# Copies of a head norm's roots one half tile ahead of their transposes, in a kernel of two transformer blocks

## The chip, the cores and the metric

The kernel runs on one core of a Trainium2 chip. The metric is device time in microseconds (us), the median of some runs. Engines are named as the profile names them: PE is TensorE (matmuls and transposes; PEld are its weight loads, which overlap the matmuls), DVE is VectorE, ACT is ScalarE, POOL is GpSimd, SP is SyncE, which issues most DMAs.

## What is computed

The reference is a first block (a causal convolution branch and an RWKV-7 branch, gated and added) and then a second block of two attention layers, each followed by a feed-forward layer with a short convolution; 16 meta tokens and 512 tokens of width 1024, batch 1, float32. The change touches the attention layers, above all the second (layer B), a differential attention. Its queries and keys are normed head by head:

```python
q1, q2 = jnp.split(h @ w_q, 2, axis=-1)
q1 = rms_norm(q1.reshape(B, Tp, N_HEADS, B_HEAD_DIM), gq)      # 8 heads of 64
q2 = rms_norm(q2.reshape(B, Tp, N_HEADS, B_HEAD_DIM), gq)
k1 = rms_norm(k1.reshape(B, Tp, N_HEADS, B_HEAD_DIM), kn_b)    # k2 the same
def attn_map(qb, kk):
    lg = jnp.einsum('bqhd,bshd->bhqs', qb, kk) * scale + bias
    return jax.nn.softmax(jnp.where(mask, lg, NEG_INF), axis=-1)
a = attn_map(q1b, k1) - lam * attn_map(q2b, k2)
```

The first attention layer (layer A) picks 256 keys for each query by an index score and has heads of 128.

## The kernel before

Activations lie transposed: 128 channels on the partitions, T = 528 tokens along the free axis, in two halves of 264 columns (`HALVES`). A projection (`gemm`, L1089) takes a weight tile of 128 x 1024 floats, which a DMA brings (`wst`), ACT casts to a high part (`wh`), and POOL subtracts to a low part (`wl`). Three products for each of 8 k tiles and each half, 48 matmuls of 264 columns, go to PSUM banks `g` or `pt`; DVE evacuates them.

Only PE's order is written by the program. The class `Weave` keeps a planner's clock: every matmul adds its cost. Before each main product `mm3` calls `tick`, which lets those streams (generators) go on that are due. A stream yields either a delay on that clock (a value of `LAT2`; in layer B `LATB` replaces some, `hd` by 8) or a condition. The other engines' instructions are ordered by a scheduler, by readiness and priority.

A head norm is such a stream (`head_norm`, L1202). It squares two tiles (ACT), sums the squares per head with small matmuls, and takes the reciprocal root (DVE, then a power on POOL), all in a tile `hn` of 88 tokens x 24 values. Then, for each of four half tiles, the roots have to come back along the tokens: with heads of 64, ACT first widens them into `hs` (88 x 384, one buffer), three transposes on PE bring them into a PSUM bank `lg` (two buffers), and DVE multiplies the tile by the gain and the bank. With heads of 128 (layer A) there is no `hs`. The only delay between half tiles is `part` (0.3 or 0.4) between the two tiles.

In layer B four query norms run while the query, key and value projections go on. Then, for each of four pairs of heads `t`, key and value projections are main products, the key norm is a stream of `keys`, and eight attention units (`unit_b`) and one for the meta tokens wait for the marks of q, k and v of that pair. Before the projections of pair `t` from 2 on, `pe.finish(*units[t - 2])` lets PE's plan wait until the units of pair t - 2 are through. In what follows q0 to q3 and k0 to k3 are the four query and key norms.

Of the kernel before, what the change touches and what calls it, by code (L numbers as in the profile page):

```python
# [22 lines left out]
TH = T // 2  # L23
# [624 lines left out]
LAT = dict(lora=4, kk=4, bonus=5, scale=4, am=1.3, inv=34, tf=8.5, merge=2.5, hop=1.5, state=3, gn=14, pivot=40, norm=60)  # L648


LAT2 = dict(acc=3, rstd=2.5, evac=2.5, sq=3, hd=6, part=0.3, soft_a=6, soft_b=4, av=1.6, qn=7, back=5, small=18, dve=1.4, rl=1.8)

LATB = dict(sq=2.5, hd=8, part=0.4, av=1.6, small=12, evac=2)
DEPTH_A, DEPTH_B = 3, 3
# [384 lines left out]
class Block2:  # L1039
# [95 lines left out]
    def rstd(self, acc, r):  # L1135

        K, nc = self.K, self.nc
        n = T // 6
        yield LAT2["acc"]
        p = self.lg()  # L1140
# [4 lines left out]
        K.rsqrt(s, s)  # L1145
        yield LAT2["rstd"]
        for j, sl in enumerate(self.HALVES):
# [23 lines left out]
    def sums(self, st):  # L1171

        K, nc = self.K, self.nc
        yield LAT2["acc"]
        p = self.lg()
# [14 lines left out]
    def start(self, rx, rb):  # L1190
        K, nc = self.K, self.nc
        M0 = N_META
        yield LAT2["rstd"]
        p = self.po()
# [7 lines left out]
    def head_norm(self, xs, width, gcol, key):  # L1202


        K, pe = self.K, self.K.pe
        n = T // 6
        per = P // width
        sel = K.k("ones")[:, 0:1] if per == 1 else K.k("bones")[:, 0:P:width]
        sqs = []
        for x in xs:  # L1210
            sqs.append(K.slot("sq"))
            K.act(sqs[-1], x, AF.Square)
        yield LAT2["sq"]
        w = 6 * per * len(xs)
        p = self.lg()
        for j, sq in enumerate(sqs):
            for b in range(6):
                o = per * (6 * j + b)
                pe.matmul(p[0:n, o:o + per], sq[:, b * n:(b + 1) * n], sel, start=True, stop=True)
        s = self.tl("hn", 2, (n, w))  # L1220
        K.ts(s, p[0:n, :w], 1.0 / width, OP.mult, 1e-6, OP.add)
        K.rsqrt(s, s)
        yield LAT2["hd"]
        for j, x in enumerate(xs):
            for q, sl in enumerate(self.HALVES):
                p = self.lg()[:, :TH]
                o = per * (6 * j + 3 * q)
                if per > 1:
                    r = self.tl("hs", 1, (n, 3, P))
                    K.nc.scalar.copy(r.rearrange("n b (h x) -> n (b h) x", h=per),  # L1230
                                     s[:, o:o + 3 * per, None].to_broadcast([n, 3 * per, width]))
                for b in range(3):
                    pe.transpose(p[:, b * n:(b + 1) * n],
                                 r[:, b] if per > 1 else s[:, o + b:o + b + 1].to_broadcast([n, P]),
                                 K.k("ident")[0:n, 0:n])
                K.stt(x[:, sl], x[:, sl], gcol, p, OP.mult, OP.mult)
            if j + 1 < len(xs):
                yield LAT2["part"]
        pe.mark(key)

    def tl(self, tag, bufs, shape=(P, T), dt=F32):
# [428 lines left out]
    def layer_b(self, hq, acc):  # L1670
# [3 lines left out]
        M0 = N_META  # L1674
        rb = K.slot("rb")
        pq = self.first(self.rstd(acc, rb), (A["w_q_b"][0], hq), (A["w_q_b"][4], hq))
        self.npT = 2
        with self.tc.tile_pool(name="ab", bufs=1, reuse_waits="tile") as self.ap:

            lv = tl("vf", 2)[:, :256]  # L1680
# [27 lines left out]
            for j in range(8):  # L1708
                t, mp = j // 2, j % 2
                p = pq[j] if j < 2 else None  # L1710
                if j == 7:
                    p = self.gemm(A["w_q_b"][t + 4 * mp], hq, both=True, bank=self.pt)
# [42 lines left out]
            acc = K.slot("acc")  # L1755
# [297 lines left out]
```

## Time and profile before

| | |
|---|---|
| median of 3 runs | 2325.27 us (2322.97 to 2329.49) |
| profiled execution | 2321.4 us, span 2319.4 us |
| PE busy | 93% of the span |
| DVE, POOL, ACT busy | 65%, 51%, 38% |
| mean granted PE clock | 0.972 of full speed |
| layer A's key norm | about 983 to 991 us |
| query norms and first key norm of layer B | about 1590 to 1681 us |
| attention units of layer B | about 1690 to 1860 us |

The profile is one execution. Its times are from the span's start. Busy shares are averages over stages with different limits; for a change in one stage the waits of that stage count. A wait in square brackets at a row's end is the idle time of that engine before the row, and what ended it.

### The profile page before, as it was taken

Reading aid. Unit: us, or ns where it says so; the run is one execution under the profiler, and the core shown is the slowest. Engines: PE = TensorE matmul, PEld = TensorE weight load, DVE = VectorE, ACT = ScalarE, POOL = GpSimd, SP = SyncE. Lnnn points to the kernel's source line nnn. Section 1 sums busy time; section 2 is a strip of 40 time slices with the busy share of each in tenths; the row PEclk is TensorE's granted clock in tenths of the full one; section 3 lists DMA queues with packets and bytes.
Section 4 is the critical chain, followed back from the end, with each engine's and each line's share of the span. In section 5 each row is a group of like instructions: output and inputs, shape, how many; then the busy total and the mean of one; then the engine's idle time right before and its main releaser. Section 6 shows DMA issues by size and latency. Waiting matters only on the chain. (4 is left out here: it accounts for less than half of the span.)

```text
span 2319.4 us, 39064 instructions
## 1 busy us (share of the span) xinstructions
PE 2167.0 (93%) x15303; PEld 1897.1 (82%) x15303; DVE 1498.8 (65%) x2693; ACT 889.9 (38%) x1762; POOL 1189.5 (51%) x993
## 2 busy tenths in 40 slices
PE   6999989997999999898999999999888999999999
PEld 4766666665777778897899999999878899988987
DVE  8478986899964377898556616632376766661661
ACT  3423233332243234435433423333375663332331
POOL 5486556475753446435454454465533345454444
PEclk9999999998999999999999999999998999999999
DMA  7422222221244745111022232232111013223223
GB/s 257 162 77 63 64 85 62 66 69 43 84 146 136 243 146 174 61 58 33 29 83 91 72 108 86 84 98 77 56 36 37 19 56 95 82 77 113 88 73 111
DMA packets 110235, 208.85 MB, mean 90 GB/s; under 512 B 45226, under 2 KB 48810, under 8 KB 110051
## 3 DMA queue, kind: packets, MB, share of 16 engines
q1 hardware_dynamic: 107072, 203.26, 28.1%
q10 hardware_dynamic: 2978, 3.10, 0.4%
q8 instruction: 120, 1.97, 0.3%
q14 instruction: 65, 0.52, 0.1%
HBM read 188.43 MB, written 20.57 MB: 90 GB/s over the span
## 5 line engine op out<-in xcount | busy, mean ns | idle before, releaser
L219 POOL TENSOR_TENSOR wl<-wst,wh 128x1024 fp32r<-128x1024 f32 (+4 forms) x315 | 706.9, 2245 | 685.0 <-ACT wh L216 552.6
L75 PE MATMUL g<-hx,wh 128*128 128x264 f32 (+3 forms) x3648 | 877.4, 330 | 0.0
L75 PEld LDWEIGHTS g<-hx,wh 128*128 128x128 f32 x3648 | 616.8, 195 | 53.0 <-issue 8.4
L75 PE MATMUL g<-hx,wl 128*128 128x264 f32 (+3 forms) x1824 | 593.0, 329 | 15.8 <-DVE u L177 7.4
L216 ACT CAST wh<-wst 128x1024 fp32r<-128x1024 f32 (+4 forms) x315 | 304.3, 966 | 375.7 <-PE g L75 207.3
L75 PEld LDWEIGHTS g<-hx,wl 128*128 128x128 f32 x1824 | 351.7, 194 | 42.2 <-DVE u L177 7.9
L177 DVE SCALAR_TENSOR_TENSOR c<-u,vec,c 128x528 f32<-128x528 f32 (+1 forms) x176 | 244.6, 1390 | 83.2 <-ACT c L180 81.6
L75 PE MATMUL pt<-hx,wh 128*128 128x264 f32 (+2 forms) x1504 | 271.9, 283 | 0.0
L177 DVE SCALAR_TENSOR_TENSOR cy<-u,vec,cy 128x512 f32<-128x512 f32 x240 | 234.4, 985 | 3.8
L75 PEld LDWEIGHTS pt<-hx,wh 128*128 128x128 f32 x1504 | 229.6, 188 | 0.0
L75 PE MATMUL pt<-hx,wl 128*128 128x264 f32 (+2 forms) x752 | 207.0, 284 | 9.9 <-DVE u L167 9.8
L75 PEld LDWEIGHTS pt<-hx,wl 128*128 128x128 f32 x752 | 138.9, 188 | 12.2 <-POOL wl L219 8.7
L75 PE MATMUL pt<-f,wh 128*128 128x264 f32 (+1 forms) x528 | 119.5, 320 | 0.0
L75 PE MATMUL g<-f,wh 128*128 128x264 f32 (+1 forms) x528 | 119.5, 320 | 0.0
L1620 ACT CAST f<-t 128x528 fp32r<-128x528 f32 (+1 forms) x44 | 27.6, 627 | 181.1 <-POOL t L167 96.0
L75 PEld LDWEIGHTS g<-f,wh 128*128 128x128 f32 x528 | 87.7, 188 | 7.1
L75 PEld LDWEIGHTS pt<-f,wh 128*128 128x128 f32 x528 | 87.7, 188 | 7.0
L167 POOL TENSOR_TENSOR t<-t,c 128x528 f32<-128x528 f32 (+1 forms) x44 | 57.6, 1310 | 66.9 <-DVE c L177 66.9
L75 PE MATMUL pt<-f,wl 128*128 128x264 f32 (+1 forms) x264 | 84.7, 321 | 2.8 <-POOL wl L219 2.8
L75 PE MATMUL g<-f,wl 128*128 128x264 f32 (+1 forms) x264 | 84.3, 319 | 0.0
L180 ACT ACTIVATE t<-c 128x528 f32<-128x528 f32 (+1 forms) x44 | 28.1, 638 | 139.9 <-DVE c L177 139.9
L167 DVE TENSOR_TENSOR f<-t,f 128x528 fp32r<-128x528 f32 (+1 forms) x44 | 35.4, 805 | 68.8 <-ACT f L1620 68.8
(417 smaller groups left out, 3918.3 us busy)
## 6 DMA issues: line engine op xcount, KB each, us to landing
wst<-in_w_up SPq DMA_DIRECT2D x88, 512.0 KB
wst<-in_w_in SPq DMA_DIRECT2D x66, 512.0 KB
ast<-in_ada_w SPq DMA_DIRECT2D x24, 512.0 KB
wst<-in_w_down SPq DMA_DIRECT2D x32, 384.0 KB
wst<-in_w_down SPq DMA_DIRECT2D x32, 320.0 KB
wst<-in_w_in_a SPq DMA_DIRECT2D x17, 512.0 KB
wst<-in_w_kv_b SPq DMA_DIRECT2D x16, 512.0 KB
wst<-in_w_conv_out SPq DMA_DIRECT2D x8, 512.0 KB
```

The costliest lines, as they stand in the source:

```text
L75: self.nc.tensor.matmul(out, lhsT, rhs, **kw)
L167: (self.nc.vector if eng == "v" else self.nc.gpsimd).tensor_tensor(out, a, b, op)
L177: self.nc.vector.scalar_tensor_tensor(out, a, s, b, op0=o1, op1=o2, accum_out=accum)
L180: self.nc.scalar.activation(out, a, f, bias=bias, scale=scale, accum_out=accum)
L216: nc.scalar.copy(wh[:, :n], st[:, :n])
L219: (nc.vector if lo == "v" else nc.gpsimd).tensor_tensor(wl[:, :n], st[:, :n], wh[:, :n], OP.subtract)
L1620: nc.scalar.copy(hi, th)
```

## The change

Each half tile now has its own delay. With `hs`, the stream first waits until no other stream holds the buffer (`self.hs`), takes it, has ACT copy, waits (8 for the first half tile, `hs` = 1.2 on the planner's clock for the others), and only then takes a bank and transposes. The buffer is given back after the transposes. Without `hs` (layer A) there is the delay of 1.2 between half tiles and no copy. `part` between the tiles is gone. The flag `self.hs` is set up in `layer_b`.

```diff
-LAT2 = dict(acc=3, rstd=2.5, evac=2.5, sq=3, hd=6, part=0.3, soft_a=6, soft_b=4, av=1.6, qn=7, back=5, small=18, dve=1.4, rl=1.8)
+LAT2 = dict(hs=1.2, acc=3, rstd=2.5, evac=2.5, sq=3, hd=6, part=0.3, soft_a=6, soft_b=4, av=1.6, qn=7, back=5, small=18, dve=1.4, rl=1.8)
@@ -1220,22 +1220,25 @@
         s = self.tl("hn", 2, (n, w))
         K.ts(s, p[0:n, :w], 1.0 / width, OP.mult, 1e-6, OP.add)
         K.rsqrt(s, s)
-        yield LAT2["hd"]
+        lat = LAT2["hd"]
         for j, x in enumerate(xs):
             for q, sl in enumerate(self.HALVES):
-                p = self.lg()[:, :TH]
                 o = per * (6 * j + 3 * q)
                 if per > 1:
+                    yield lambda: not self.hs
+                    self.hs = True
                     r = self.tl("hs", 1, (n, 3, P))
                     K.nc.scalar.copy(r.rearrange("n b (h x) -> n (b h) x", h=per),
                                      s[:, o:o + 3 * per, None].to_broadcast([n, 3 * per, width]))
+                yield lat
+                lat = LAT2["hs"]
+                p = self.lg()[:, :TH]
                 for b in range(3):
                     pe.transpose(p[:, b * n:(b + 1) * n],
                                  r[:, b] if per > 1 else s[:, o + b:o + b + 1].to_broadcast([n, P]),
                                  K.k("ident")[0:n, 0:n])
+                self.hs = False
                 K.stt(x[:, sl], x[:, sl], gcol, p, OP.mult, OP.mult)
-            if j + 1 < len(xs):
-                yield LAT2["part"]
         pe.mark(key)
@@ -1674,7 +1677,7 @@
         M0 = N_META
         rb = K.slot("rb")
         pq = self.first(self.rstd(acc, rb), (A["w_q_b"][0], hq), (A["w_q_b"][4], hq))
-        self.npT = 2
+        self.npT, self.hs = 2, False
```

Two places of PE's order show it. The first is q0, the first query norm: `lg<-con,hs` are its transposes, `g<-hx,wl` and `g<-hx,wh` the products. Before:

```order
L75 MATMUL g<-hx,wh 128x264 x2
L79 MATMUL lg<-con,hs 128x88 x6
L75 MATMUL g<-hx,wl 128x264
L75 MATMUL g<-hx,wh 128x264 x2
L75 MATMUL g<-hx,wl 128x264
L79 MATMUL lg<-con,hs 128x88 x6
L75 MATMUL g<-hx,wh 128x264 x2
```

and now:

```order
L75 MATMUL g<-hx,wh 128x264 x2
L79 MATMUL lg<-con,hs 128x88 x3
L75 MATMUL g<-hx,wl 128x264
L75 MATMUL g<-hx,wh 128x264 x2
L75 MATMUL g<-hx,wl 128x264
L75 MATMUL g<-hx,wh 128x264 x2
L75 MATMUL g<-hx,wl 128x264
L75 MATMUL g<-hx,wh 128x264 x2
L75 MATMUL g<-hx,wl 128x264
L75 MATMUL g<-hx,wh 128x264
L79 MATMUL lg<-con,hs 128x88 x3
```

Two groups of six transposes have become four groups of three, and eleven products stand between the first two of them.

The second place is PE at the second boundary of layer B: the last units of the first head pair and the first unit of the second (`lg<-ks` are its scores, `pt<-con,vf` transposes of values, `po<-V,pT` the products with the values). Before:

```order
L79 MATMUL pt<-con,vf 128x128 x4
L79 MATMUL pt<-con,vf 16x128
L75 MATMUL lg<-ks,qh 128x144
L75 MATMUL lg<-ks,ql_15684 128x144
L75 MATMUL g<-hx,wh 128x264
L75 MATMUL g<-hx,wl 128x264
L75 MATMUL g<-hx,wh 128x264
L79 MATMUL pt<-con,vf 128x128 x4
L79 MATMUL pt<-con,vf 16x128
L75 MATMUL lg<-ks,qh 128x144
```

and now:

```order
L79 MATMUL pt<-con,lg 128x128 x4
L79 MATMUL po<-con,lg 128x128
L75 MATMUL po<-V,pT 128x128 x5
L79 MATMUL pt<-con,vf 128x128 x4
L79 MATMUL pt<-con,vf 16x128
L79 MATMUL pt<-con,os 128x128
L75 MATMUL po<-V,pT 128x128 x5
L79 MATMUL pt<-con,vf 128x128 x4
L79 MATMUL pt<-con,vf 16x128
L79 MATMUL pt<-con,om 128x16 x2
L75 MATMUL lg<-ks,qh 128x144
L75 MATMUL lg<-ks,ql_15684 128x144
```

The last units of the first pair have moved behind the products that stood among them; these rows are part of 52 instructions without a product.

## Rows read from the trace of the kernel before

**Rows 1.** The page, busy us of each engine, share of span, instructions.

```profile
PE 2167.0 (93%) x15303; PEld 1897.1 (82%) x15303; DVE 1498.8 (65%) x2693; ACT 889.9 (38%) x1762; POOL 1189.5 (51%) x993
```

**Rows 2.** The tile hs: copies (ns min/median/max), and who waited for them (us, times).

```profile
L1230 ACT COPY hs<-hn x32: 493/510/513, 1596.2 to 1847.5; 88x384 f32<-88x384 f32 x32
...
  PEld lg L79: 19.4, 23
```

**Rows 3.** Timeline of q0: start us, us, engine, what, [idle before <-releaser].

```profile
1596.17 0.50 ACT L1230 COPY hs<-hn 88x384 f32<-88x384 f32 x1
...
1600.25 0.39 PE L79 MATMUL lg<-con,hs 88*128 88x88 f32 x3
...
1600.44 1.04 ACT L216 CAST wh<-wst 128x1024 fp32r<-128x1024 f32 x1 [3.78 <-PE g L75]
...
1601.39 0.51 ACT L1230 COPY hs<-hn 88x384 f32<-88x384 f32 x1
...
1601.96 0.45 PE L79 MATMUL lg<-con,hs 88*128 88x88 f32 x3 [1.32 <-ACT hs L1230]
...
1604.16 0.70 PE L79 MATMUL lg<-con,hs 88*128 88x88 f32 x3 [0.66 <-ACT hs L1230]
```

**Rows 4.** PE by stretch: us, PE busy (instructions), granted clock, DMA share, GB/s.

```profile
1600.00:1605.00 5.00, 2.90 (x22) 0.87 0.21 78
1605.00:1615.00 10.00, 10.00 (x59) 0.56 0.16 50
...
1625.00:1630.00 5.00, 5.00 (x36) 0.75 0.00 0
...
1645.00:1650.00 5.00, 4.97 (x39) 0.70 0.26 98
...
1658.00:1663.00 5.00, 3.30 (x28) 1.00 0.00 0
1663.00:1676.00 13.00, 13.00 (x117) 1.00 0.28 88
1676.00:1681.00 5.00, 2.89 (x24) 1.00 0.25 90
sum 91.00, PE 80.60; mean PE 6.20
```

**Rows 5.** Timeline of q2, the third norm, POOL, DVE and PE.

```profile
1641.55 2.37 POOL L219 TENSOR_TENSOR wl<-wst,wh 128x1024 fp32r<-128x1024 f32 x1 [3.32 <-issue]
...
1641.83 2.65 DVE L177 SCALAR_TENSOR_TENSOR hx<-h,vec,hx 128x528 fp32r<-128x528 f32 x1
...
1645.03 0.67 PE L79 MATMUL lg<-con,hs 88*128 88x88 f32 x3 [1.13 <-DVE qx L177]
```

**Rows 6.** Waits for hs from 1700 to 1860; then PE by stretch.

```profile
  PEld lg L79: 6.3, 8
...
1796.00:1800.00 4.00, 4.00 (x27) 0.72 0.00 0
...
1850.00:1855.00 5.00, 5.00 (x33) 0.72 0.00 0
```

**Rows 7.** PE in one stretch of the attention units.

```profile
1700.00:1850.00 150.00, 131.40 (x985) 0.92 0.09 29
```

**Rows 8.** Two long waits of PE among the units, and the clock behind each.

```profile
1774.47 1.08 PE L79 MATMUL pt<-con,lg 128*128 128x128 f32 x4 [3.00 <-DVE lg L177]
...
1775.00:1785.00 10.00, 10.00 (x57) 0.52 0.12 48
...
1739.81 0.28 PE L79 MATMUL pt<-con,vf 128*16 128x128 f32 x1 [2.17 <-DVE qx L177]
...
1740.00:1745.00 5.00, 5.00 (x31) 0.66 0.35 108
```

**Rows 9.** Layer A's key norm: busy of PE, PEld, DVE, ACT, POOL, then clock.

```profile
985.00:990.00 5.00, 1.80 (x9) 1.54 (x10) 5.00 (x19) 0.00 (x0) 0.14 (x1) 0.58 0.33 107
990.00:995.00 5.00, 5.00 (x33) 5.00 (x33) 5.00 (x22) 1.57 (x4) 0.00 (x0) 0.73 0.00 0
```

## The prediction

> **What bounds the kernel now.** The page comes first: TensorE (PE) is busy 93% of the span, with 15303 matmuls [rows 1]. PE is the engine whose waits have to be found, and an idle moment of another engine costs nothing until PE waits for it. Then I asked for the tile `hs`, the widened roots that the change is about. Its 32 copies take 0.51 us each, and PE's weight loads waited for them 23 times, 19.4 us in all [rows 2]. The timeline of the first norm shows how one such wait is made [rows 3]. The first copy is done at 1596.7, long before its transposes at 1600.25, so one half tile in four is already hidden. The second copy can start only when the first transposes have read the one buffer; ACT is in a weight cast by then (1600.44, 1.04 us), the copy runs at 1601.39, and PE's next instruction, the next three transposes, stands still for 1.32 us. With ACT free the same wait is 0.66 us.
>
> The third view is a table by stretch of the stage in which the four query norms and the first key norm (k0) fall [rows 4]. From 1590 to 1681 PE is busy 80.60 of 91.00 us, so 10.40 us idle, and every idle stretch holds a norm; between norms PE is full (13.00 of 13). The table shows a second cost. [...] Busy time times the missing share: 10 x 0.44 = 4.4, 5 x 0.25 = 1.25, 4.97 x 0.30 = 1.5, 2.90 x 0.13 = 0.4; together 7.5 us. In this stage, then, 10.4 + 7.5 = 17.9 us hang on the norms.
>
> **The change, part by part.** No instruction is added or taken away: 32 copies, 96 transposes of these tiles and 32 evacuations stay, and SP and POOL keep their order there. What moves is PE's order. Where six transposes stood together, three stand now, then some eleven products, then three. Cover: 117 PE instructions take 13.00 us in [rows 4], 0.111 us each, so eleven give 1.2 us. To be covered is 0.66 us with a free ACT, 1.32 us behind a cast [rows 3]. So a copy on a free ACT is hidden with 0.5 us to spare, and one behind a full cast leaves about 0.1 us. The casts come when a product's buffers are released, which is not at every half tile.
>
> *Query norms and k0.* One wait is not a wait for a copy. In the third norm PE stood 1.13 us for the evacuation of an earlier half (DVE qx), because DVE was in a hx operation that took 2.65 us beside POOL's wl split of 2.37 us [rows 5]. The new order does not touch that, so I keep 1.1 us there, and half of the 1.5 us of low clock behind it, 0.7. Gain: 17.9 - 1.8 = 16.1 us. Bounds: 17.9 if everything goes, and 9 if only the waits on a free ACT go and the clock falls as before.
>
> [...]
>
> *Key norms k1 to k3.* These run among the attention units. PE's loads waited 6.3 us there for copies, and behind k2 and k3 the clock is 0.72 over 4 and 5 us: 0.28 x 9 = 2.5 us. Together 8.8 us [rows 6]. But here PE idles for other reasons too: 150.0 - 131.4 = 18.6 us from 1700 to 1850 [rows 7], of which the copies are a third. The rest waits for chains of softmax, which do not become shorter when PE comes to them sooner. What is late next is such a chain. I take half, 4.4 us; ends 0 and 8.8.
>
> *What the new lock costs.* A stream holds the buffer from its first copy to its last transposes, and the 8 us of delay in the plan now count from getting it. So the fourth query norm starts only when the third is through, and k0 after that. In the order of before k0's last transposes stand at row 5513 of PE, now at 5563, some fifty rows of products later. The units of the first head pair wait for k0. They start later, while the products meanwhile run on. At the second boundary (the third pair's projections wait until the first pair's units are done) the products are used up: 52 PE instructions of units stand there without a product between them; in the order of before products stand between. How long PE waits there the trace of before can't show. From below: nothing, if the 52 instructions cover each other's chains. From above, the longest unit wait: 3.00 us for DVE's lg at 1774.47, followed by 10 us at clock 0.52, which costs 4.8 us; 7.8 us in all. A middle row: 2.17 us at 1739.81 and 5 us at 0.66, 1.7 us; 3.9 us in all [rows 8]. The new place has one short softmax (144 and 272 keys) after another, as that middle row has, so I take 4.
>
> *Layer A.* The key norm there has one head per tile: no copy, but its halves are now spread as well. PE lost 3.2 us there and 2.1 us of clock (1.80 x 0.42 + 5 x 0.27), yet DVE is busy 5.00 of 5 there [rows 9]: DVE's top-k work sets the pace, and PE would arrive earlier only to wait. I take 0; ends 0 and 5.
>
> Sum: 16.1 + 4.4 - 4 = 16.5 us. The profiled execution took 2321.4 us, 3.9 us under the median of 2325.27: 2304.9 by the one, 2308.8 by the other. I take **2307**.
>
> **The rivals.**
> 1. *More is won.* The key norms give back all of their 8.8 us and the boundary hides: 17.9 + 8.8 = 26.7, 2298 from the median. For it: the copies' waits are PE's own. Against: [rows 7].
> 2. *The units give it back.* The boundary costs 7.8 us, and the key norms give nothing: 16.1 - 7.8 = 8.3, 2317. For it: the 52 rows without a product. Against: it is one place only.
> 3. *The clock stays low.* The falls could come from the transposes and not from the waits; then only idle time is won. In rows: 10.4 - 1.1 = 9.3, less 4 at the boundary, plus 3.1 of the key norms' waits: 8.4, 2317. Against it: the norms in 1658 to 1663 and 1676 to 1681 have the same twelve transposes at clock 1.00 [rows 4]. [...]
> 4. *It doesn't do what it says.* The copies stand behind casts and the lock makes the streams queue, so that PE waits at three of four half tiles still. Half of the waits and half of the clock go: 9, less 4: 5, 2320.
> 5. *Slower.* The later k0 shifts all units, and products run out at each of the three boundaries between head pairs, each at 7.8 us: 23.4 against 16.1 won, and the key norms' 0: 7.3 us slower, 2333. It decides from 16.1 / 3 = 5.4 us a boundary on. Against it: the order shows a long stretch without products at one boundary; at the others they are as long as before.
>
> **How the numbers follow.** A measurement of this kernel can tell about 0.3%, 7 us, from no change; so faster means under 2318.3, slower over 2332.2. The forecast has 0.55 (2300 to 2313, its unknowns at their bounds); more 0.10; units 0.13 (0.08 of it under 2318.3); clock 0.07 (0.04); not as it says 0.09 (0.02); slower 0.06 (0.04 of it over 2332). Faster: 0.55 + 0.10 + 0.08 + 0.04 + 0.02 = 0.79. Slower 0.04. The rest, 0.17, is within. The range reaches from 2296, most of "more", to 2320, which takes in 2, 3 and half of 4, and leaves out 5: 2296 to 2320.
>
> **What would show it.** Right: the waits of PE's loads for `hs` fall from 19.4 us to a few; from the first to the fifth norm PE is busy over 97% and the clock stays at 1.00, so that this stage is some 16 us shorter; a wait for DVE or ACT of some us at the second boundary, with a lower clock behind it. Wrong: the same stage no shorter, or PE waits of copies that now stand behind casts; the attention units longer by more than 8 us; or a stage outside these two that changed, since no order changed there.

## The result, and the profile after

The changed kernel took 2298.7 us (median; 2293.82 to 2301.47), the kernel before 2328.2 us in runs beside it. The ratio is 0.987 (0.985 to 0.989): 29.5 us faster, where 18 were forecast. The profiled execution took 2293.8 us with a span of 2292.0 us, against 2319.4 us. That is inside the range that I gave (2296 to 2320), near its lower end, but not in the 2300 to 2313 of the forecast itself, to which I had given 0.55; of the cases named, the nearest is the first rival, "more is won" (2298), to which I had given 0.10. Two runs at a far lower clock are left out below: one of the changed kernel (2930.95 us, clock 0.65) and one of the kernel before (2630.16 us, 0.74).

The page's first line answers to [rows 1]: the same 15303 matmuls, 15 us less of PE's busy time, and the other engines as they were.

```profile
PE 2151.7 (94%) x15303; PEld 1885.8 (82%) x15303; DVE 1496.7 (65%) x2693; ACT 888.0 (39%) x1762; POOL 1187.3 (52%) x993
```

The same work at the lower clock is longer busy time: in the kernel before, the product `g<-hx,wl` takes 285 ns on the mean from 1663 to 1676 (clock 1.00) and 423 from 1606 to 1614 (0.51). So most of these 15 us are clock. The mean granted clock went from 0.972 to 0.977, and the missing share of the two spans, 65 and 53 us, differs by some 12 us.

The tile `hs` in the changed kernel, to be set against [rows 2]: first why an engine stood idle before work on `hs` (its releaser, us, times), then who waited for it.

```profile
  PE lg L79: 20.2, 14
...
  PEld lg L79: 0.2, 1
```

Before, PE's loads waited 19.4 us for copies; now PE waits once, 0.2 us. ACT, which has time, still waits for PE to give the buffer back, 20.2 us in all, as it did before (14.5 us, 14 times). The timeline of PE in q0 shows PE's side, beside [rows 3] (start, us, what, and no square bracket where PE did not wait):

```profile
1601.88 0.39 PE L79 MATMUL lg<-con,hs 88*128 88x88 f32 x3
...
1603.59 0.45 PE L79 MATMUL lg<-con,hs 88*128 88x88 f32 x3
...
1606.71 0.43 PE L79 MATMUL lg<-con,hs 88*128 88x88 f32 x3
...
1608.36 0.39 PE L79 MATMUL lg<-con,hs 88*128 88x88 f32 x3
```

To compare whole stages between kernels I cut them at fixed events: the *query norms* run from the first evacuation of a query projection to the first one of a value projection, the *units* from there to the first product of the output projection. k0, whose end [rows 4] counts with the norms, falls into the units here. PE by these two stretches (us, PE busy and instructions, granted clock, DMA share, GB/s), in the kernel before:

```profile
1582.00:1668.10 86.10, 77.81 (x618) 0.90 0.19 57
1668.10:1855.30 187.20, 164.18 (x1244) 0.93 0.11 34
```

and in the changed one:

```profile
1583.00:1651.20 68.20, 68.20 (x614) 1.00 0.21 67
1651.20:1824.90 173.70, 154.60 (x1251) 0.98 0.12 39
```

The query norms are full: not one idle moment, clock 1.00, 17.9 us shorter. The units are 13.5 us shorter: idle 23.0 to 19.1 us, and time lost to the lower clock (busy time times the missing share of the granted clock) 11.5 to 3.1 us. The first output products behind them are 2.2 us longer (47.0 to 49.2), layer A 2.0 us shorter (234.1 to 232.1). Each of the other stretches became longer by less than 3 us, 3.9 us together.

### The profile page after: what moved, and what is told of

Same layout as the page of the kernel before. It is cut to its first block, busy times and chain, and to the rows that moved or that the text cites. A ratio compares the mean times of both kernels' runs of the same rounds, so it can differ in the third digit from the quotient of the medians.

```text
span 2292.0 us, 39075 instructions
## 1 busy us (share of the span) xinstructions
PE 2151.7 (94%) x15303; PEld 1885.8 (82%) x15303; DVE 1496.7 (65%) x2693; ACT 888.0 (39%) x1762; POOL 1187.3 (52%) x993
## 5 line engine op out<-in xcount | busy, mean ns | idle before, releaser
L75 PEld LDWEIGHTS g<-hx,wh 128*128 128x128 f32 x3648 | 609.6, 193 | 53.3 <-issue 8.6
L177 DVE SCALAR_TENSOR_TENSOR c<-u,vec,c 128x528 f32<-128x528 f32 (+1 forms) x176 | 244.5, 1389 | 83.3 <-ACT c L180 81.6
L177 DVE SCALAR_TENSOR_TENSOR cy<-u,vec,cy 128x512 f32<-128x512 f32 x240 | 233.7, 982 | 3.8
L167 POOL TENSOR_TENSOR t<-t,c 128x528 f32<-128x528 f32 (+1 forms) x44 | 57.5, 1308 | 67.0 <-DVE c L177 67.0
L167 DVE TENSOR_TENSOR f<-t,f 128x528 fp32r<-128x528 f32 (+1 forms) x44 | 35.4, 805 | 68.7 <-ACT f L1623 68.7
```

What stands on the lines that cost most here:

```text
L75: self.nc.tensor.matmul(out, lhsT, rhs, **kw)
L167: (self.nc.vector if eng == "v" else self.nc.gpsimd).tensor_tensor(out, a, b, op)
L177: self.nc.vector.scalar_tensor_tensor(out, a, s, b, op0=o1, op1=o2, accum_out=accum)
```

## Experiments

Twelve kernels ran. The stages come from one trace each; a ratio is to the kernel before on the same chip, with its 95% interval. The last column is the time that PE's loads waited for the tile `hs`. In e1, e6, e8 and e11 only the key norms use `hs`; the query norms' copies go to other tiles there.

| kernel | median us | ratio | query norms | units | waits |
|---|---|---|---|---|---|
| before | 2325 to 2329 | | 86.1 | 187.2 | 19.4 |
| changed | 2298.7 | 0.987 (0.985 to 0.989) | 68.2 | 173.7 | 0.2 |
| a2, changed again | 2293.6 | 0.987 (0.981 to 0.992) | 67.6 | 177.1 | 0.2 |
| e1, four buffers | 2311.6 | 0.992 (0.989 to 0.995) | 73.7 | 184.3 | 9.0 |
| e2, query norms alone | 2303.5 | 0.988 (0.983 to 0.994) | 68.1 | 175.9 | 8.1 |
| e3, key norms alone | 2311.6 | 0.993 (0.990 to 0.996) | 88.1 | 171.4 | 10.9 |
| e4, layer A alone | 2321.7 | 0.997 (0.994 to 1.000) | 88.1 | 184.3 | 19.4 |
| e5, no products between | 2332.2 | 1.003 (1.000 to 1.005) | 90.9 | 186.1 | 23.9 |
| e6, no lock | 2299.8 | 0.988 (0.984 to 0.993) | 74.1 | 167.9 | 0.6 |
| e7, late k0 alone | 2317.2 | 0.996 (0.994 to 0.998) | 86.2 | 175.9 | 21.7 |
| e8, lock for queries alone | 2296.0 | 0.986 (0.983 to 0.989) | 68.5 | 171.4 | 0.6 |
| e9, splits on DVE in before | 2317.9 | 0.995 (0.993 to 0.998) | 79.8 | 173.7 | 19.2 |
| e10, half the delay | 2312.7 | 0.994 (0.991 to 0.997) | 81.4 | 182.4 | 7.9 |
| e11, e8 with splits on DVE | 2288.9 | 0.984 (0.982 to 0.986) | 67.5 | 166.6 | 0.3 |

**e1: the waits go, the clumps stay.** In the kernel before, each query norm gets four buffers (tiles that the units use later), and its four copies run ahead; PE's order stays.

```diff
+        rs, ahead = [], key[0] == "q"
+        for o in range(0, 12 * per, 3 * per) if ahead else ():
+            r = self.tl("lg", 6)[0:n, 0:3 * P].rearrange("n (b x) -> n b x", b=3)
+            K.nc.scalar.copy(...)
+            rs.append(r)
...
+                if ahead:
+                    r = rs[2 * j + q]
```

> The kernel before, with its PE order kept instruction for instruction; only the four widened copies of a query norm go to four different buffers and are all made before the first transposes (key norms as before). The twelve transposes still stand six and six. If the waits for the copies are what costs in the query norms and what lowers the clock behind them, PE's idle time in the stage of the norms falls by 6 to 8 us (a little stays where a third group waits for a bank), the clock behind q0, q1 and q2 stays at 1.00 (7.5 us), and the kernel is 12 to 16 us faster than before. If it is the clumped transposes that lower the clock, it falls behind q0 to q2 as before, and the gain is 6 to 8 us. The attention units keep their order, so by either theory their stage stays as long as before, within 3 us.

The query norms took 73.7 us, with 2.5 us idle and 1.4 us lost to the clock. PE by stretch in that kernel, around three of its norms:

```profile
1605.00:1612.00 7.00, 6.65 (x66) 1.00 0.36 89
1620.00:1626.00 6.00, 6.00 (x53) 1.00 0.31 87
1636.00:1642.00 6.00, 4.32 (x37) 1.00 0.39 94
1642.00:1650.00 8.00, 7.54 (x58) 0.79 0.17 63
```

Twelve transposes stand together as before, and the clock is 1.00 through them; it falls only in the last row, behind the 1.79 us for which PE stood for DVE's qx. So in this trace twelve transposes together did not bring the clock down; where it fell in this stage, it fell behind a wait. My third rival falls, and without the copies' waits this trace has 12.4 of the 17.9 us of the query norms (how much of that is clock varies, see e9). In time e1 is 17 us faster than before, a little over the 12 to 16 expected. Most of what is left over against the changed kernel is the qx wait, which spread transposes hide as well.

**e2, e3, e4: one part alone.** The new form holds for one kind of norm, the old one (behind the same lock) for the others.

```diff
+        if key[0] == "q":          # e2; "kn" in e3; per == 1 in e4
+            (the changed form)
+        else:
+            (the form before)
```

> The new form for the four query norms alone; key norms and layer A in the old form (the keys still wait for the buffer). The first key norm still comes late, behind q3. If the gain in the units comes from their later start and other order, this kernel has most of it: 24 to 30 us faster than before. If it comes from the products between the key norms' transposes, it has only the query norms' part: 14 to 18 us faster.

> The new form for the four key norms alone. If the products between the key norms' transposes give the units' gain: 2 us at k0 and 9 to 11 us in the units, 11 to 13 us faster than before. If the order behind a late k0 gives it: 2 to 6 us faster, the waits of PE's loads for hs among the units gone all the same.

> Only layer A's key norm has its half tiles spread; layer B as before. DVE is full there, so within 2 us of the kernel before (between -2 and 0); if PE's lost 5 us there were on the path, 4 to 5 us faster.

In time e2 is 25 us faster than before and e3 17, together more than the whole change; e3's gain is over both of its expectations. The query norms alone give all of the 18 us in their stage, and 8 to 11 us in the units that they do not touch (175.9, against 187.2 in before and 184.3 in e4, which has the same order there). The key norms alone bring the units to 171.4 us, 13 to 16 us less. The two gains in the units do not add: together they give 7 to 13.5. So the units hold something that quite different new orders of PE take away, though not every one (e5 and e10 below). In e2 it isn't a late k0, as its expectation has it: 8 fewer products stand before k0's last transposes in PE's order than in the kernel before, where the change has 48 more. Layer A's part is 7 us by the medians, 0.3%, with an interval from 0.6% to nothing; its stage took 229.8 to 233.8 us in the eight traces with layer A spread (232.1 in the mean) and 234.1 to 236.7 in the six without (235.2), so 3 us.

**e5: the lock without products.** The delay between half tiles is 0 in layer B. The lock and the copies ahead stay. k0 is not late here: 4 fewer products stand before its last transposes than in the kernel before.

```diff
-                lat = LAT2["hs"]
+                lat = LAT2["hs"] if per == 1 else 0.0
```

> The changed kernel with the delay between half tiles of layer B at 0 in place of 1.2: the lock and the early first copy stay, but all twelve transposes of a norm stand together in PE's order again. If the products between them are what hides the copies, the stage of the query norms is as long as before (86 to 88 us from the first query evacuation to the first value evacuation, against 68 of the changed kernel), PE's loads wait some 20 us for hs, and the kernel is within 6 us of the kernel before, less or more what the other order of the units does. If the lock and the order alone did it, the stage is 68 to 72 us.

Nothing is won: 90.9 us of query norms, 23.9 us of waits. A copy that is written ahead is of no use with nothing for PE to do behind it. The order of the units is new here too, but they stay long (186.1): PE stood 4.57 us for DVE's os, whose input stood in POOL's queue behind a key norm's power of 4.17 us.

**e10: half of the products.** `hs=0.6` for 1.2.

> The change with half the delay between half tiles (0.6 for 1.2 on the planner's clock): five to seven products between, 0.6 to 0.75 us of cover. Theory (cover against a copy of 0.66 us on a free ACT, 1.32 us behind a cast, the arithmetic of the prediction): copies on a free ACT just hidden, those behind a cast or a square leave 0.5 us and more each, 2 to 4 us of hs waits in all in layer B, norm stage 68 to 72 us, and 2298 to 2304. Rival (any product between is enough, or the lock alone): no hs wait over 0.3 us, norm stage 68. With all cover gone the stage took 90.9 us.

The waits are there, but more than expected (7.9 us, where I wrote 2 to 4), and so is the stage (81.4, of which 4.4 idle and 6.9 of clock). ACT in q3 (`sq<-k` is a square of k0, which stands between) and PE's transposes show why a cover of half the size is worth less than half:

```profile
1657.27 1.05 ACT L216 CAST wh<-wst 128x1024 fp32r<-128x1024 f32 x1 [6.61 <-PE g L75]
1658.23 0.50 ACT L1231 COPY hs<-hn 88x384 f32<-88x384 f32 x1
...
1659.18 1.04 ACT L216 CAST wh<-wst 128x1024 fp32r<-128x1024 f32 x1
1660.12 0.64 ACT L180 ACTIVATE sq<-k 128x528 f32<-128x528 f32 x1
1660.66 0.50 ACT L1231 COPY hs<-hn 88x384 f32<-88x384 f32 x1
```

```profile
1658.79 0.45 PE L79 MATMUL lg<-con,hs 88*128 88x88 f32 x3 [0.55 <-ACT hs L1231]
1661.21 0.45 PE L79 MATMUL lg<-con,hs 88*128 88x88 f32 x3 [1.21 <-ACT hs L1231]
```

A copy stands behind a cast (a wait of 0.55 us), or behind a cast and a square (1.21). With the whole cover 0.2 us of such waits was left in the changed kernel; half of it hides neither form, and behind the longer wait the clock falls to 0.50 (1664.3 to 1668.3). The rest of the loss is in the units (182.4 us): they have three waits of over 3 us, two of them behind a DVE operation of 2.36 and 2.39 us beside a split, of the kind that e9 below is about. This trace is one of the slowest executions of e10 (2319.4 against a median of 2312.7).

**e6 and e8: what the lock does.** In e6 there is no lock: the query norms' copies go to tiles of the later units, the key norms keep `hs`. e8 is the same with the lock among the query norms alone.

```diff
-                    yield lambda: not self.hs
-                    self.hs = True
-                    r = self.tl("hs", 1, (n, 3, P))
+                    if key[0] == "q":          # e8: with the lock here
+                        r = self.tl("lg", 6)[0:n, 0:3 * P].rearrange("n (b x) -> n b x", b=3)
+                    else:
+                        r = self.tl("hs", 1, (n, 3, P))
...
-                self.hs = False                # e8: kept for the queries
```

> The changed kernel without the queue at the buffer: the query norms' copies go to other buffers (those of the unit scores, unused there), so no stream waits for another; all delays as in the change. The stage of the query norms as in the changed kernel (68 us). The order has no 52 instructions without a product at the second boundary. If that stretch costs 4 us or more as I forecast, the units are 4 to 8 us shorter than the changed kernel's 174 us; if it costs little, they are the same within 3 us.

> The change, but the lock is among the query norms alone: their copies go to tiles of the later units, the key norms keep hs to themselves, so k0 need not wait for q3. Theory (the lock is of use among the queries, where without it q1's first transposes stood 3.79 us for their roots, and the late k0 that it brings costs the units 6 to 9 us: 167.9 us without the lock, 173.7 and 177.1 with it): norm stage 68 us, no idle; units 168 us; some 6 us under the change, 2293. Rival (the units' time is set by how the streams happen to fall between the products, and a late k0 costs nothing by itself): norm stage 68, units anywhere from 171 to 177, 2296 to 2302, no difference from the change that can be told.

Without the lock the query norms take 74.1 us, with one wait of 3.79 us. POOL, ACT and PE of that kernel, one row each from their timelines:

```profile
1611.61 4.15 POOL L185 TENSOR_TENSOR hn<-hn,mhalf 88x24 f32<-88x24 f32 x1 [1.36 <-DVE hn L174]
...
1615.79 2.16 ACT L1232 COPY lg<-hn 88x384 f32<-88x384 f32 x5 [1.89 <-POOL hn L185]
...
1616.77 0.45 PE L79 MATMUL lg<-con,lg 88*128 88x88 f32 x3 [3.79 <-ACT lg L1232]
```

q1's roots wait for POOL's power (4.15 us), and PE comes to its transposes before them. With the lock q1 queues behind q0 and its roots are there: 68.5 us in e8. So among the query norms the lock, which I had put down as a cost alone, is worth some 6 us. For k0 it seems to cost something: units 167.9 and 171.4 us without it, 173.7 and 177.1 with it. The times don't show it: the medians are 2296.0 against 2298.7 and 2293.6. e8's 171.4 us and 2296.0 are what its rival expected, not the theory (168 and 2293), so the size of that cost stays open between nothing and some 6 us.

**e7: the late k0 alone.** In the kernel before, k0's stream is held back by 6.3 on the planner's clock.

```diff
+        if t == 0:
+            yield 6.3
```

> The kernel before with one delay added: the first key norm starts 6.3 us later on the planner's clock, so that the units start as late as in the changed kernel and the stretch without products at the second boundary is there as well. The query norms are untouched (86 to 88 us). If the late start costs, the units take 188 to 195 us, against 184 to 187 of the order before; if the late start is what made the units shorter in the changed kernel, they take 172 to 178 us.

The units became shorter (175.9), although PE still waited 21.7 us for copies. A delay that does nothing but move the units against the products gains 8.7 us over the runs of before beside it. What it took away is the wait of 3.00 us in [rows 8], with the low clock behind it: no wait in that trace's units is over 2.14 us. In the kernel before, two such DVE operations (`lg`, `ql`) took 2.94 and 2.37 us there; in e7 no operation of the same two lines (L177, L167) takes over 1.4 us in the units.

**e9: the cause of that wait.** PE's order is that of before, instruction for instruction. The 14 splits (`wl`) of the value weights and of the second to fourth pair's key weights go from POOL to DVE.

```diff
-                    self.proj(A["w_kv_b"][t + 4 * mp], hk, rb, None, 0, pk[mp], kt[:, mp])
+                    pk_ = pk[mp] if t == 0 else self.gemm(A["w_kv_b"][t + 4 * mp], hk, lo="v")
+                    self.proj(A["w_kv_b"][t + 4 * mp], hk, rb, None, 0, pk_, kt[:, mp])
...
+                                self.gemm(A["w_kv_b"][8 + 2 * t + j], hk, lo="v")) for j in range(2)]
```

> The kernel before with PE's order as it was; the splits (wl) of the second to fourth pair's key weights and of all value weights run on DVE and not on POOL, 14 splits. Theory (PE's long waits among the units come from DVE operations with two SBUF inputs held up beside a POOL split, 2.94 us for 0.75 at 1771.38 and 2.37 for 0.42 at 1737.12, and the low clock comes from these waits): the waits of 3.00 and 2.17 us and the clock of 0.50 behind them go; DVE's own splits of about 1.3 us each put back a part; units 176 to 181 us for 184 to 187, 2318 to 2322. Rival (the waits are DVE's load and the softmax chains, whatever POOL does): DVE gets some 18 us more, units 187 to 195, 2328 to 2336. Waits for hs stay 23 times, 19 us, by both.

The kernel before, around the 3.00 us: DVE and POOL, from their timelines.

```profile
1771.38 2.94 DVE L177 SCALAR_TENSOR_TENSOR lg<-lg,rs 128x528 f32<-128x528 f32 x1
...
1771.42 2.34 POOL L219 TENSOR_TENSOR wl<-wst,wh 128x1024 fp32r<-128x1024 f32 x1 [0.49 <-ACT wh L216]
```

DVE's operation started 0.04 us ahead of the split and took 2.94 us. The wait of 2.17 us stands behind another such pair: DVE's ql took 2.37 us from 1737.12 on, beside a split of 2.36 us from 1736.86 on. The same forms on DVE over the whole of the units (busy us, mean ns), before:

```profile
L167 DVE TENSOR_TENSOR ql<-qx,qh 64x256 fp32r<-64x256 f32 x24 | 13.6, 566 | 1.6 <-ACT qh L1836 1.3
...
L177 DVE SCALAR_TENSOR_TENSOR lg<-lg,rs 128x528 f32<-128x528 f32 x6 | 6.8, 1131 | 0.1
```

and with the splits on DVE:

```profile
L219 DVE TENSOR_TENSOR wl<-wst,wh 128x1024 fp32r<-128x1024 f32 x11 | 13.5, 1224 | 2.3 <-ACT wh L216 2.2
L167 DVE TENSOR_TENSOR ql<-qx,qh 64x256 fp32r<-64x256 f32 x24 | 10.0, 416 | 1.6 <-ACT qh L1838 1.3
...
L177 DVE SCALAR_TENSOR_TENSOR lg<-lg,rs 128x528 f32<-128x528 f32 x6 | 4.6, 763 | 0.1
```

DVE has 13.5 us more to do in the units, and the kernel is 8.6 us faster: with PE's order unchanged, the wait of 3.00 us of [rows 8] is gone (0.04 us at the same instruction), and that of 2.17 us is 1.05. These waits belong to the order and not to one execution: e1 and e4, whose units have the order of before, have them again (2.99 and 2.16; 3.00 and 2.16). What counted here is not DVE's load but when it was held: `lg` took 2.94 us beside the split, and 0.76 us on the mean in e9. In the two pairs of before DVE started 0.04 us ahead of the split and 0.26 us after it, and ended 0.56 and 0.27 us behind it. An operation that reads a bank was not held in the same trace: `qx<-g,rb` took 0.43 us at 1597.53, within a split of 2.40 us from 1595.86 on, and all twelve of its kind 0.42 to 0.43. Why DVE was held, these times don't show. The profiled execution of e9 is one of its quickest (2305.5 against a median of 2317.9), so its 173.7 us of units show more than the median gains. Its query norms are a warning about e1: PE waits at the same nine places as in before (7.8 us of idle time for 8.3), but the clock falls behind q0 alone, and the stage loses 1.4 us to it for 7.8 in before (busy time times the missing share). PE by stretch in e9, around its second norm (waits of 0.66 and 0.66 us), where the clock fell in [rows 4]:

```profile
1621.50:1625.50 4.00, 2.56 (x22) 1.00 0.46 131
1625.50:1629.50 4.00, 4.00 (x41) 1.00 0.00 0
```

**e11: both.** e8 with e9's splits on DVE; PE's order is e8's.

> The kernel with the lock among the query norms alone (2296.0), and in it the 14 splits of the key and value weights on DVE; PE's order is that kernel's. Theory (the two causes add: in that kernel PE stood 3.14 us for a DVE operation of 2.36 us, ql, beside a split of 2.34 us, and the clock behind it was 0.50; the splits on DVE took the like away in the order of before and were worth 8.6 us there, more than 1 us of them in the norm stage, which is full here): norm stage 68 to 69 us, the wait of 3.14 us and the clock of 0.50 behind it gone, units 164 to 168 us for 171.4, time 2288 to 2293. Rival (with the norms spread PE is so full that DVE's added 14 x 1.22 = 17 us of splits are late for the softmax chains, and the waits only move): units 169 to 174, 2294 to 2300.

e8's longest wait had the same cause: DVE's ql took 2.36 us beside a split of 2.34 us, PE stood 3.14 us, and the clock behind it was 0.50. In e11 DVE is no longer late there (ql 0.41 us); PE stands 2.16 us at the same instruction, now for ACT's V. PE by stretch:

```profile
1584.80:1652.30 67.50, 67.50 (x610) 1.00 0.25 72
1652.30:1818.90 166.60, 153.11 (x1252) 0.98 0.13 39
```

2288.9 us is the best time here, 7.1 us under e8, and it lies below the lowest run of e8 (2290.97) and of the changed kernel (2290.01). The two were measured on different chips; against the runs of before beside each, the gain is 35.7 us in e11 and 30.5 in e8, and the intervals of the ratios overlap, so 5 to 7 us is an estimate.

## Why the prediction was right, and where it was off

**The mechanism was right.** Copies ahead with products between end PE's waits for `hs` (19.4 to 0.2 us), and the clock in the query norms is 1.00. e5 and e1 show both halves: without products nothing is won, and with the copies' waits gone the clock stays at 1.00 but behind one wait (1.79 us, for qx). The clock is also 1.00 in the five traces whose query norms are spread behind the lock (the change twice, e2, e8, e11).

**The query norms: 16.1 us of idle time and clock went, 14.0 were forecast for them** (16.1 less 2.1 for k0, which falls into the units here); the other 1.8 us of the stage's 17.9 is less busy time of PE, of which the four instructions fewer (618 to 614) account for some 0.4 at 0.111 us each; where the rest went stays open. The step that failed is the 1.8 us that I kept for q2 in [rows 5]. DVE is still held beside splits in that stage (of eight hx operations one takes 2.43 us at 1627.38 and one 2.14 at 1633.87, the others 0.76), but with the transposes spread, PE has products in hand while DVE is late. "The new order does not touch that" was wrong: the cover hid the late evacuation as well as the late copies. One bound was misread: I gave 9 us for "only the waits on a free ACT", but in the trace of before the waits of 0.66 us or less add up to 3.9 us there, and all waits for copies to 8.8.

**The units: 13.5 us (10.1 in the second trace) against a forecast of 2.5** (k0's 2.1 and 4.4, less 4). Against e4, whose units have the order of before and took 184.3 us, it is 10.6 and 7.2. This is the term that made the forecast too cautious, by 5 to 11 us. Three steps are in it:

- *Half of the key norms' 8.8 us.* The copies' waits are all gone, not half.
- *The boundary, 4 us.* The number held, as far as it can be read, but not all of the reason. PE by stretch at the second boundary of the changed kernel:

```profile
1705.00:1710.00 5.00, 3.33 (x27) 1.00 0.00 0
1710.00:1715.00 5.00, 4.31 (x36) 1.00 0.00 2
1715.00:1720.00 5.00, 2.19 (x17) 1.00 0.35 107
1720.00:1725.00 5.00, 3.98 (x27) 0.77 0.00 0
1725.00:1730.00 5.00, 5.00 (x37) 0.89 0.02 5
```

  From 1705 to 1725 PE idles 6.2 us, and the clock takes 1.5 us more up to 1730: 7.7 us. Twenty average us of the units before cost 20 x 34.5 / 187.2 = 3.7 us of both kinds, so the place costs 4 us more than average, an estimate from these rows; the second trace has 5.8 and 4.2 us there, so 6. PE waits for ACT's V (2.06 us, the longest) and DVE's mx (1.17). Short chains one after another were forecast, but the longest wait is in part something else: ACT's copy of V stood behind an operation on os that waited 0.78 us for DVE, and os stood behind DVE's ql, which took 2.37 us at 1712.94 beside a split of 2.35 us on POOL (1712.68).
- *The waits of [rows 8].* Here the reasoning failed. I read 3.00 and 2.17 us, with 4.8 and 1.7 us of low clock behind them, as prices for a new wait, and let the waits themselves stand in the sum. They were 11.7 us of the units, and they were no property of the softmax chains but collisions: a DVE operation and a POOL split that happened to start together. e7 removed the larger by moving the units, e9 by moving the split. A change that shifts the streams throws these dice again, and before had a bad throw (e10 has another). So this part of the gain was luck as far as the forecast goes: nothing in its reasoning says that the new order would throw better. The changed kernel has held operations of this kind still (DVE's ql of 2.37 us at 1712.94 and of 2.29 at 1744.40), yet no wait of PE over 2.06 us in the units.

**Rivals.** "More is won" named the right place for the surplus, the key norms, but only part of its cause. "The units give it back" and "slower" needed dear boundaries; one costs 4 to 6 us net. "It doesn't do what it says" asked for copies behind casts: that is e10, at half the delay. **Layer A** gave about 3 us where I took 0, within my ends of 0 and 5. In its key norm PE waited 3.84 us for DVE's k before (2.98 and 0.86) and waits 2.81 now, so DVE still sets the pace there, as I wrote; where the rest came from stays open.

**Outside these stages** the first output products became 2.2 us longer, in both traces of the changed kernel (49.2 us, against 47.0 in before and 47.0 to 48.2 in all the others); 1.6 us of it is waiting, the longest new wait 1.18 us for DVE's qx. No term of the forecast held this. The rest moved by no more than traces differ.

## What to carry to other kernels

Put work of the bound engine between a hand-off and its use, as much as the helper's longest queue (here a cast, a square and a copy), and check the clock behind each wait: nearly half of the gain here was clock, by the estimate below. Before pricing a new order, look at the longest waits of the old one and ask whether they are chains or collisions of two engines, which here moved with the order (e7) and could be taken away at their root (e9). A queue for a buffer is not only a cost: it held a stream back until its data were there (74.1 us of query norms in e6, 68.5 in e8).

## What the runs showed of the hardware

Here the clock did not follow from the waits alone. The changed kernel ran twice with a trace. Both times PE stood for DVE's k at the same place, 1.66 and 1.65 us. PE behind it in the first:

```profile
1694.00:1698.00 4.00, 2.92 (x24) 1.00 0.18 72
1698.00:1702.00 4.00, 3.75 (x30) 1.00 0.01 4
```

and in the second, 2.7 us earlier on the span:

```profile
1692.00:1696.00 4.00, 2.71 (x20) 0.95 0.03 11
1696.00:1700.00 4.00, 4.00 (x20) 0.50 0.02 4
1700.00:1704.00 4.00, 3.34 (x19) 0.70 0.00 0
```

The second went to 0.50, the first stayed at 1.00, and this place alone is about 3 us, an estimate from these rows. e9 and the kernel before differ in the same way behind their second norm. Over 68 runs of the kernel before, the mean granted clock lay between 0.960 and 0.975 and the time between 2344 and 2316 us, 18.5 us for each 0.01 of clock (correlation -0.93). The mean clock of the kernel before was 0.969 over these, that of the changed kernel 0.976 over its six: by that line 13 us, nearly half of the 29.5, are clock. What decides between two equal waits stays open.
